# RWKV recurrence: block-diagonal state, zero-padded inverses and chunk products on alternate halves of the columns

## The chip, the cores and the metric

The kernel runs on one core of a Trainium2 chip. The metric is the device time of one execution in microseconds; lower is better. Each time is a median of several executions.

## The reference

The model has two transformer-like layers (a mixer and a feed-forward part each), and then two more layers of other kinds. It works on 512 tokens of width 1024. The mixer of each of the first two layers is made of three parts that read the same projection: RWKV7, retention, and latent attention. The change is in RWKV7, which has 4 heads of 64 channels and this recurrence over the tokens:

```
def step(state, inp):
    rt, kt, vt, wt, kkt, at = inp
    sa = jnp.einsum('bhvk,bhk->bhv', state, -kkt)
    state = (state * wt[:, :, None, :] + sa[..., None] * (kkt * at)[:, :, None, :]
             + vt[..., None] * kt[:, :, None, :])
    return state, jnp.einsum('bhvk,bhk->bhv', state, rt)
```

The output of a token is a matrix-vector product with a 64x64 state of each head; the state decays by channel, loses what an old key held, and gains the new value.

## The kernel before

The recurrence is computed in 8 chunks of 64 tokens (`CH`, `NCH`). Channels of two heads stand on the 128 partitions: head 2p + e is in tile p, on partitions 64e to 64e + 63. `rwkv_front` makes, for each chunk, `ar` (removal keys and receptances, scaled by decays) and `bk` (their counterparts), each 64 channels by 2 x 64 columns for a head.

- `rwkv_scores` forms, for each chunk and head, the 128x128 masked score matrix `g` of bk and ar (tile gps, 64 rows by 128 columns; the four products of one bank have the same e). It sends the 32x32 diagonal blocks to DRAM (SP's and POOL's queues), and transposes bk (`bkt`) and the values (`uv`) to token-major form.
- `rwkv_inverse` inverts 32 strictly lower triangular 64x64 matrices: a substitution of 31 steps on VectorE in 32x32 blocks, a way through DRAM (`s2`, then `tt`: 4 DMAs, two from SP's queue and two from ScalarE's), and a merge in four groups (tile mrg: 32x32 products, all in rows 0 to 63 and columns 0 to 31).
- `rwkv_chunk` runs 8 times in order. bch = scores x values + ar x state; copy to SBUF; uch = inverse x bch; copy into `uv`; mch = bkt x uv, from which with the decay `gam` the next state (`mst`) is made; ych = output. The products are in float32, for which each matmul stands as two instructions in the trace. bch and uch put all heads on output partitions 0 to 63; the products with the state use 64 rows (the head's channels), the others 128. mch and ych put heads of e = 0 and e = 1 on alternate halves of the output partitions.

All this runs beside the other two parts of the mixer. In `attn` the helper `weave` emits, after each step of `main` (retention, latent attention), 1.9 steps of `side` (scores, inverse, chunks), with a priority of 600 (`SPRI`). A scheduler orders each engine's queue before the run from priorities and a model of costs; engines then run their queues in order. Tiles of one tag share slots: tag R, with 26 slots of 128x512, holds most of the recurrence's tiles. Banks of PSUM have the tags pd, pt, pr and pa with two each; the recurrence uses pr. Dense products (tile pd, line 366) split weights and activations into a high and a low part, in three products each.

Of the kernel before, what the change touches and what calls it, by code (L numbers as in the profile page):

```python
# [5 lines left out]
F32 = mybir.dt.float32  # L6
# [9 lines left out]
P = 128  # L16
T = 512
# [19 lines left out]
# how far ahead of the program's order: loads and splits of weights, of small ones, products leaving their banks,  # L37
# reciprocal roots, the recurrence
WPRI, SMPRI, EPRI, CPRI, SPRI = 300, 0, 200, 500, 600
# first loads: block of x before which the second unit of weights comes, rank of the splits, who squares and adds blocks of x  # L40
START, AHEAD, VSQ, VACC = 3, -300, (5, 7), (6,)
# attention: steps of the recurrence per step beside it; steps of the retention after which latent values and queries follow;
# steps of the latent attention by which values wait, queries come early, and after which the recurrence's output follows; banks
WEAVE, VAT, QAT, VDELAY, QAHEAD, RPOST = 1.9, (2, 6, 10, 14), 6, 1, 3, 20
MSCB, MOB, DB0, DB1, DB2 = ("pa", "pr", "pa", "pr"), "pd", ["pd", "pt"], ["pd"], ["pd"]
# end of the even layer: products after which weights of the odd layer are split, places of the sums and roots, delay of the fourth product
EARLY, SEAM, LATE, AH2, AH3 = (3, 5), (3, 1, 5, 5, 1), 2, -300, -250
# odd layer: steps of the gates after each product, steps of what runs beside values and output gates
# [28 lines left out]
def _constants():  # L77
# [34 lines left out]
    # decays of the retention, split between queries and keys about the middle token  # L112
# [16 lines left out]
def _layout(inp):  # L129
    """Every array as the chip reads it; only permutations, slices, copies and zero padding."""  # L130
# [15 lines left out]
    for l in range(L2):  # L146
# [10 lines left out]
        # retention's values beside the latent keys' rotary part, three blocks of rows to a unit  # L157
# [61 lines left out]
class _Kernel:  # L219
# [7 lines left out]
    def t(self, name, tag, dt=F32):  # L227
        """a [128, T] tile; tags share slots in the order in which their tiles are written first"""
        if tag in KEPT:
            return self.tp.tile([P, T], dt, tag=tag, name=name, bufs=KEPT[tag])  # L230
        return self.php.tile([P, T], dt, tag=tag, name=name, bufs=self.phb[tag])

    def phase(self, name, **tags):
        """memory of one phase: tag -> number of [128, T] slots"""
# [21 lines left out]
    def pd(self, name="pd"):  # L256
        """a bank for a dense product, in turn from the tags that the phase has set aside"""
        self.turn += 1
        return self.bank(self.dbanks[self.turn % len(self.dbanks)], name)
# [70 lines left out]
    def wbits(self, src, tags, n=UNIT, ahead=0):  # L330
        """a unit of weights in tiles of the phase: (k, columns) -> (hi, lo)"""
# [28 lines left out]
    def evac(self, out, ps, y):  # L360
        """a dense product times y, ahead of other work so that its bank is free again"""
# [6 lines left out]
    def mm3(self, out, a, b, first, last):  # L368
        """out += a^T b, both operands as exact (hi, lo) pairs."""
# [21 lines left out]
    def rsqrt_(self, x, n, key, bias, more, floor):  # L391
# [12 lines left out]
        # a step of third order, then one of Newton's  # L404
# [11 lines left out]
    def col_sums(self, ps, c0, sq, rhs, first=True, last=True):  # L416
        """ps[:, c0 + tb*n ...] = sum over partitions of sq, token-major."""
# [4 lines left out]
    def spread(self, r, ps):  # L422
        """r: [128 tokens, token blocks] -> psum [128 features, tokens]"""
# [4 lines left out]
    def spread_heads(self, r, ps, tag):  # L428
        """r: [128 tokens, token blocks * two heads] -> psum [64 features of each head, T]"""
# [49 lines left out]
    def softplus(self):  # L479
        """4 softplus(-lam)"""  # L480
# [24 lines left out]
    def rope_angles(self):  # L505
        """cos and sin of both rotations, on [32 * token block + frequency, token], kept in DRAM as
# [1323 lines left out]
```

## Time and profile before

| | |
|---|---|
| time, median of 3 runs | 2117.26 us (2115.75 to 2122.51) |
| profiled execution, span (its only time) | 2118.6 us |
| TensorE busy | 98% |
| VectorE, ScalarE, GpSimd busy | 60%, 38%, 3% |
| granted TensorE clock, mean | 0.961 |

A TensorE clock of 1.00 is 2.4 GHz and 0.50 is 1.2 GHz. In rows, `128*64 128x64` means a stationary operand of 128 rows and 64 columns and a moving one of 128 rows by 64; PE is TensorE's matmul part, DVE is VectorE, ACT is ScalarE, SP is the queue of SyncE. Matmuls are pipelined: the length of one runs on under the next, so the step from start to start is what one costs.

### The profile page before, as it was taken

Reading aid. Unit: us, or ns where it says so; the run is one execution under the profiler, and the core shown is the slowest. Engines: PE = TensorE matmul, PEld = TensorE weight load, DVE = VectorE, ACT = ScalarE, POOL = GpSimd, SP = SyncE. Lnnn points to the kernel's source line nnn. Section 1 sums busy time; section 2 is a strip of 40 time slices with the busy share of each in tenths; the row PEclk is TensorE's granted clock in tenths of the full one; section 3 lists DMA queues with packets and bytes.
Section 4 is the critical chain, followed back from the end, with each engine's and each line's share of the span. In section 5 each row is a group of like instructions: output and inputs, shape, how many; then the busy total and the mean of one; then the engine's idle time right before and its main releaser. Section 6 shows DMA issues by size and latency. Waiting matters only on the chain.

```text
span 2118.6 us, 25896 instructions
## 1 busy us (share of the span) xinstructions
PE 2086.5 (98%) x10080; PEld 1662.8 (78%) x10080; DVE 1277.1 (60%) x2387; ACT 805.6 (38%) x1315; POOL 66.1 (3%) x112
## 2 busy tenths in 40 slices
PE   8999999999999999999999999999999999999998
PEld 5787667888888877776678888888788888878786
DVE  7963176553544678623755445346988885388565
ACT  6421164322322444213643223225554544347242
POOL 3100000000000011000000000000000000020000
PEclk9986699999999999958999999999999999999999
DMA  5320022332333333201222323333333323222121
GB/s 184 107 64 13 28 59 74 97 96 93 100 100 96 124 113 105 64 5 32 67 88 92 100 91 98 100 95 90 98 96 93 102 95 103 101 69 90 50 90 40
DMA packets 64782, 180.06 MB, mean 85 GB/s; under 512 B 13764, under 2 KB 16612, under 8 KB 64660
## 3 DMA queue, kind: packets, MB, share of 16 engines
q1 hardware_dynamic: 60464, 175.27, 26.9%
q0 software_dynamic: 1808, 2.69, 0.5%
q8 instruction: 79, 1.29, 0.3%
q10 hardware_dynamic: 2388, 0.45, 0.2%
q14 instruction: 43, 0.35, 0.1%
HBM read 172.29 MB, written 6.09 MB: 84 GB/s over the span
## 4 chain that ended last, share of the span: by engine, by line
PE 45%; DVE 4%; ACT 2%; DMA 1%; issue 1%; DVEq 0%; ACTq 0%
PE pd L366 39%; PE egate L366 1%; PE mo L366 1%; DVE wl L285 1%; PE oo L366 1%; PE msc L366 1%; PE ost L366 1%; DVE xl L303 0%; ACT wh L306 0%; DVE h L285 0%; PE osb L366 0%; ACT oe L306 0%; PE osf L366 0%; PE mpt L1145 0%; DMA wr<-ewin 0%
## 5 line engine op out<-in xcount | busy, mean ns | idle before, releaser
L366 PE MATMUL pd<-xh,wh 128*128 128x512 f32 (+1 forms) x1512 | 591.6, 391 | 6.4 <-ACT xh L306 6.4
L366 PE MATMUL pd<-xl,wh 128*128 128x512 f32 (+1 forms) x1512 | 592.8, 392 | 4.4 <-DVE xl L303 3.9
L366 PE MATMUL pd<-xh,wl 128*128 128x512 f32 (+1 forms) x1512 | 589.9, 390 | 0.0
L306 ACT ACTIVATE wh<-wr 128x1024 fp32r<-128x1024 f32 (+3 forms) x285 | 296.4, 1040 | 763.4 <-PE pd L366 524.5
L285 DVE TENSOR_TENSOR wl<-wr,wh 128x1024 fp32r<-128x1024 f32 (+3 forms) x285 | 341.7, 1199 | 102.0 <-ACT wh L306 100.8
L366 PEld LDWEIGHTS pd<-xl,wh 128*128 128x128 f32 (+1 forms) x1512 | 284.0, 188 | 67.2 <-DVE xl L303 8.6
L366 PEld LDWEIGHTS pd<-xh,wh 128*128 128x128 f32 (+1 forms) x1512 | 284.2, 188 | 65.5 <-ACT xh L306 7.2
L366 PEld LDWEIGHTS pd<-xh,wl 128*128 128x128 f32 (+1 forms) x1512 | 284.1, 188 | 57.6 <-issue 1.0
L366 PE MATMUL pd<-fal,wh 128*128 128x512 f32 x352 | 137.2, 390 | 0.0
L366 PE MATMUL pd<-fah,wl 128*128 128x512 f32 x352 | 137.0, 389 | 0.0
L366 PE MATMUL pd<-fah,wh 128*128 128x512 f32 x352 | 136.6, 389 | 0.0
L285 DVE TENSOR_TENSOR h<-pd,h 128x512 f32<-128x512 f32 x64 | 44.2, 691 | 150.1 <-PE pd L366 150.1
L366 PE MATMUL pd<-mxh,wh 128*128 128x512 f32 (+1 forms) x272 | 102.8, 378 | 0.0
L366 PE MATMUL pd<-mxh,wl 128*128 128x512 f32 (+1 forms) x272 | 102.6, 377 | 0.0
L366 PE MATMUL pd<-mxl,wh 128*128 128x512 f32 (+1 forms) x272 | 102.5, 377 | 0.0
L285 DVE TENSOR_TENSOR fth<-pd,RH 128x512 f32<-128x512 f32 x44 | 30.4, 692 | 118.6 <-PE pd L366 118.6
L285 DVE TENSOR_TENSOR fz<-pd,RB 128x512 f32<-128x512 f32 x44 | 30.4, 692 | 99.3 <-PE pd L366 99.3
L366 PEld LDWEIGHTS pd<-fal,wh 128*128 128x128 f32 x352 | 66.1, 188 | 14.3 <-DVE fal L285 0.6
L366 PEld LDWEIGHTS pd<-fah,wl 128*128 128x128 f32 x352 | 66.1, 188 | 13.7
L366 PEld LDWEIGHTS pd<-fah,wh 128*128 128x128 f32 x352 | 66.1, 188 | 13.6
L366 PEld LDWEIGHTS pd<-mxl,wh 128*128 128x128 f32 x272 | 51.2, 188 | 9.3
L366 PEld LDWEIGHTS pd<-mxh,wl 128*128 128x128 f32 x272 | 51.2, 188 | 9.2
(507 smaller groups left out, 3038.3 us busy)
## 6 DMA issues: line engine op xcount, KB each, us to landing
wr<-wgu SPq DMA_DIRECT2D x88, 512.0 KB, 3.5
wr<-ewin SPq DMA_DIRECT2D x48, 512.0 KB, 3.5
wr<-win SPq DMA_DIRECT2D x35, 512.0 KB, 3.5
wr<-wd SPq DMA_DIRECT2D x32, 512.0 KB, 3.6
wr<-wout SPq DMA_DIRECT2D x16, 512.0 KB, 3.5
wr<-ewout SPq DMA_DIRECT2D x16, 512.0 KB, 3.8
wr<-wd SPq DMA_DIRECT2D x16, 384.0 KB, 3.2
h<-xT SPq DMA_DIRECT2D x16, 256.0 KB, 4.7
```

Source lines behind the costliest of these rows:

```text
L285: (eng or self.nc.vector).tensor_tensor(out, x, y, op)
L306: self.nc.scalar.activation(out, x, f, **kw)
L366: self.nc.tensor.matmul(out=out, lhsT=lhsT, rhs=rhs, start=start, stop=stop)
```

## The change

The state of two heads becomes a block-diagonal 128x128 tile (`mbd`, two of them in turn), whose other blocks are set to zero once a layer. The inverses lie in `tt` with the heads of e = 0 on partitions 0 to 63 and those of e = 1 on 64 to 127, and the other half is zero. Thereby every product of a chunk has 128 rows by 64 columns, and successive products belong to e = 0 and e = 1, on alternate halves of the output partitions. bch has one bank and one copy; uch's result is copied in two halves, on VectorE and on ScalarE. The new state is (mch + state) x decay, in two adds and two multiplies of 64 partitions. The scores of e = 0 and e = 1 alternate, in two banks. `tt` comes back from DRAM in 8 DMAs, and the merge takes all 16 matrices of each e at once, the two e in alternation on different corners of the array, with three tiles of tag R. The diff also drops comments and docstrings everywhere; its core:

```diff
+        st = {"v": [], "ar": [], "bk": [], "rk": []}
+        st["gam"] = self.s("gam", 2 * NCH)[:].rearrange("p (c q) -> p c q", q=2)
...
-            g = self.s(f"gam{p}", NCH)
-            nc.vector.tensor_copy(g, e1[:].rearrange("p (c t) -> p c t", t=CH)[:, :, CH - 1])
-            st["gam"].append(g)
+            nc.vector.tensor_copy(st["gam"][:, :, p], e1[:].rearrange("p (c t) -> p c t", t=CH)[:, :, CH - 1])
...
+    def rwkv_memory(self, st):
+        st["tt"] = self.php.tile([P, 32, CH], F32, tag="tt", name="tt", bufs=1)
+        self.nc.gpsimd.memset(st["tt"], 0.0)
+        st["mbd"] = []
+        for i in range(2):
+            m = self.php.tile([P, 2 * P], F32, tag=f"mbd{i}", name="mbd", bufs=1)
+            self.nc.gpsimd.memset(m, 0.0)
+            st["mbd"].append(m[:].rearrange("p (q v) -> p q v", v=P))
     def rwkv_scores(self, l, st):
         nc = self.nc
         s1 = self.dr.tile([2, 32, 32, 32], F32, tag="s1", name="s1")
         st["g"] = []
         mask = self.co("mg").unsqueeze(1).to_broadcast([P, 4, P])
+        self.rwkv_memory(st)
         for cp in range(NCH // 2):
-            row = []
-            for e in range(2):
-                sl = slice(64 * e, 64 * e + 64)
-                ps = self.pr("gps")
-                for i in range(4):
-                    c, p = 2 * cp + i // 2, i % 2
+            row, pss = [], [self.pr("gps") for _ in range(2)]
+            for i in range(4):
+                c, p = 2 * cp + i // 2, i % 2
+                for e in range(2):
+                    sl = slice(64 * e, 64 * e + 64)
                     lh = st["bk"][p][c // 4][sl, c % 4].rearrange("p s t -> p (s t)")
                     rh = st["ar"][p][c // 4][sl, c % 4].rearrange("p s t -> p (s t)")
-                    self.mm(ps[:, i * P:(i + 1) * P], lh, rh, True, True)
+                    self.mm(pss[e][:, i * P:(i + 1) * P], lh, rh, True, True)
+            for e in range(2):
                 g = self.t("g", "R")
                 g3 = g[:].rearrange("p (h t) -> p h t", t=P)
-                self.mul(g3, ps[:].rearrange("p (h t) -> p h t", t=P), mask)
+                self.mul(g3, pss[e][:].rearrange("p (h t) -> p h t", t=P), mask)
                 row.append(g3)
                 for b, q in enumerate((nc.sync, nc.gpsimd)):
                     d = slice(32 * b, 32 * b + 32)
-                    q.dma_start(out=s1[b, 8 * cp + 4 * e:8 * cp + 4 * e + 4].rearrange("h j t -> j h t"), in_=g3[d, :, d])
+                    m = 16 * e + 4 * cp
+                    q.dma_start(out=s1[b, m:m + 4].rearrange("h j t -> j h t"), in_=g3[d, :, d])
...
-        tt = self.php.tile([P, 32, CH], F32, tag="tt", name="tt", bufs=1)
-        nc.gpsimd.memset(tt[32:64, :, 0:32], 0.0)
+        tt = st["tt"]
         s2 = self.dr.tile([P, 16, 32], F32, tag="s2", name="s2")
         nc.sync.dma_start(out=s2, in_=x3)
-        for hf in range(2):
-            for b, q in enumerate((nc.sync, nc.scalar)):
-                o, i = 64 * hf + 32 * b, 32 * b + 16 * hf
-                q.dma_start(out=tt[i:i + 16, :, 32 * b:32 * b + 32], in_=s2[o:o + 32].rearrange("c i t -> i c t"))
-        tts = [tt[:, 8 * g:8 * g + 8] for g in range(4)]
-        st["tt"] = tts
-        for g in range(4):
-            n21 = self.php.tile([P, 256], F32, tag="q1k", name="n21", bufs=3)
-            n3 = n21[:, :256].rearrange("p (c t) -> p c t", t=32)
-            t11 = self.php.tile([P, 256], F32, tag="q1k", name="t11", bufs=3)
-            t3 = t11[:, :256].rearrange("p (c t) -> p c t", t=32)
-            for e in range(2):
-                nc.vector.transpose(out=n3[32:64, 4 * e:4 * e + 4], in_=st["g"][g][e][0:32, :, 32:64])
-            nc.vector.transpose(out=t3[0:32], in_=tts[g][0:32, :, 0:32])
-            ps = self.pr("mrg")
-            for i in range(8):
-                self.mm(ps[0:32, 32 * i:32 * i + 32], n3[32:64, i], tts[g][32:64, i, 32:64], True, True)
-            w = self.php.tile([P, 256], F32, tag="q1k", name="mrgw", bufs=3)
-            self.act(w[0:32, :256], ps[0:32, :256])
-            ps = self.pr("mrg2")
-            for i in range(8):
-                self.mm(ps[0:32, 32 * i:32 * i + 32], t3[0:32, i], w[0:32, 32 * i:32 * i + 32], True, True)
-            self.act(tts[g][0:32, :, 32:64], ps[0:32, :256].rearrange("p (c t) -> p c t", t=32))
-            yield
+        for e in range(2):
+            for hf in range(2):
+                for b, q in enumerate((nc.sync, nc.scalar)):
+                    o, i = 64 * hf + 32 * b + 16 * e, 64 * e + 32 * b + 16 * hf
+                    q.dma_start(out=tt[i:i + 16, 16 * e:16 * e + 16, 32 * b:32 * b + 32], in_=s2[o:o + 16].rearrange("c i t -> i c t"))
+        n21 = self.t("n21", "R")[:].rearrange("p (c t) -> p c t", t=32)
+        t11 = self.t("t11", "R")[:].rearrange("p (c t) -> p c t", t=32)
+        w = self.t("mrgw", "R")[:].rearrange("p (c t) -> p c t", t=32)
+        half = [(slice(64 * e, 64 * e + 32), slice(64 * e + 32, 64 * e + 64), slice(16 * e, 16 * e + 16)) for e in range(2)]
+        for e, (up, dn, own) in enumerate(half):
+            for g in range(4):
+                nc.vector.transpose(out=n21[dn, 4 * g:4 * g + 4], in_=st["g"][g][e][0:32, :, 32:64])
+            nc.vector.transpose(out=t11[up], in_=tt[up, own, 0:32])
+        pss = [self.pr("mrg") for _ in range(2)]
+        for i in range(16):
+            for e, (up, dn, own) in enumerate(half):
+                self.mm(pss[e][up, 32 * i:32 * i + 32], n21[dn, i], tt[dn, 16 * e + i, 32:64], True, True)
+        for e, (up, dn, own) in enumerate(half):
+            self.act(w[up], pss[e][up].rearrange("p (c t) -> p c t", t=32))
+        yield
+        pss = [self.pr("mrg2") for _ in range(2)]
+        for i in range(16):
+            for e, (up, dn, own) in enumerate(half):
+                self.mm(pss[e][up, 32 * i:32 * i + 32], t11[up, i], w[up, i], True, True)
+        for e, (up, dn, own) in enumerate(half):
+            self.act(tt[up, own, 32:64], pss[e][up].rearrange("p (c t) -> p c t", t=32))
+        yield
 
     def rwkv_chunk(self, l, st, c):
         nc = self.nc
         if c == 0:
             st["y"] = [self.t("yrw", "R"), self.t("yrw", "R")]
-            st["m"] = None
-        UV, TT = st["uv"][c], st["tt"][c // 2]
-        G = [[st["g"][c // 2][e][:, 2 * (c % 2) + p] for p in range(2)] for e in range(2)]
-        M = st["m"]
-        b = self.php.tile([P, 256], F32, tag="q1k", name="bsb", bufs=3)
-        for e in range(2):
-            sl = slice(64 * e, 64 * e + 64)
-            ps = self.pr("bch")
-            for p in range(2):
-                h = 2 * p + e
-                o = ps[0:64, p * 64:p * 64 + 64]
-                self.mm(o, G[e][p][:, 0:64], UV[:, h * 64:h * 64 + 64], True, M is None)
-                if M is not None:
-                    self.mm(o, st["ar"][p][c // 4][sl, c % 4, 0], M[sl, p, :], False, True)
-            nc.vector.tensor_copy(b[0:64, e * P:e * P + P], ps[0:64, :P])
+        UV, first = st["uv"][c], c == 0
+        M, Mn = st["mbd"][c % 2], st["mbd"][(c + 1) % 2]
+        sl = [slice(0, 64), slice(64, 128)]
+        def G(p, e):
+            return st["g"][c // 2][e][:, 2 * (c % 2) + p]
+        def V(p, e):
+            return UV[:, (2 * p + e) * 64:(2 * p + e) * 64 + 64]
+        ps = self.pr("bch")
+        for p in range(2):
+            o = slice(p * 64, p * 64 + 64)
+            for e in range(2):
+                self.mm(ps[sl[e], o], G(p, e)[:, 0:64], V(p, e), True, first)
+            if not first:
+                for e in range(2):
+                    self.mm(ps[sl[e], o], st["ar"][p][c // 4][:, c % 4, 0], M[:, p, sl[e]], False, True)
+        b = self.php.tile([P, P], F32, tag="q1k", name="bsb", bufs=2)
+        nc.vector.tensor_copy(b, ps[:, :P])
         ps = self.pr("uch")
-        for h in range(4):
-            p, e = divmod(h, 2)
-            self.mm(ps[0:64, h * 64:h * 64 + 64], TT[0:64, 4 * e + 2 * (c % 2) + p], b[0:64, e * P + p * 64:e * P + p * 64 + 64], True, True)
-        nc.vector.tensor_copy(UV[0:64], ps[0:64, :256])
+        for p in range(2):
+            for e in range(2):
+                self.mm(ps[sl[e], p * 64:p * 64 + 64], st["tt"][:, 16 * e + 2 * c + p], b[:, p * 64:p * 64 + 64], True, True)
+        uv3 = UV.rearrange("p (q e v) -> p q e v", e=2, v=64)
+        p3 = ps[:, :P].rearrange("p (q v) -> p q v", v=64)
+        nc.vector.tensor_copy(uv3[0:64, :, 0], p3[0:64])
+        self.act(uv3[0:64, :, 1], p3[64:128])
         if c < NCH - 1:
             ps = self.pr("mch")
-            for h in range(4):
-                p, e = divmod(h, 2)
-                self.mm(ps[64 * e:64 * e + 64, p * 64:p * 64 + 64], st["bkt"][p][c // 4][:, c % 4, 64 * e:64 * e + 64],
-                        UV[:, h * 64:h * 64 + 64], True, True)
-            Mn = self.sp.tile([P, 2, 64], F32, tag="mst", name="mst")
             for p in range(2):
-                gm = st["gam"][p][:, c:c + 1]
-                if M is None:
-                    self.ts(Mn[:, p], ps[:, p * 64:p * 64 + 64], gm)
-                else:
-                    mg = self.sp.tile([P, 64], F32, tag=f"mg{p}", name="mg")
-                    self.ts(mg, M[:, p], gm)
-                    self.stt(Mn[:, p], ps[:, p * 64:p * 64 + 64], gm, mg, ALU.mult, ALU.add)
-            st["m"] = Mn
+                for e in range(2):
+                    self.mm(ps[sl[e], p * 64:p * 64 + 64], st["bkt"][p][c // 4][:, c % 4, 64 * e:64 * e + 64], V(p, e), True, True)
+            p3 = ps[:, :P].rearrange("p (q v) -> p q v", v=64)
+            gm = st["gam"][:, c].unsqueeze(2).to_broadcast([P, 2, 64])
+            if first:
+                for e in range(2):
+                    self.mul(Mn[sl[e], :, sl[e]], p3[sl[e]], gm[sl[e]])
+            else:
+                new = self.sp.tile([P, 2, 64], F32, tag="mst", name="mst")
+                for e in range(2):
+                    self.add(new[sl[e]], p3[sl[e]], M[sl[e], :, sl[e]])
+                for e in range(2):
+                    self.mul(Mn[sl[e], :, sl[e]], new[sl[e]], gm[sl[e]])
         ps = self.pr("ych")
-        for h in range(4):
-            p, e = divmod(h, 2)
-            sl = slice(64 * e, 64 * e + 64)
-            o = ps[sl, p * 64:p * 64 + 64]
-            self.mm(o, UV[:, h * 64:h * 64 + 64], G[e][p][:, 64:128], True, M is None)
-            if M is not None:
-                self.mm(o, M[sl, p, :], st["ar"][p][c // 4][sl, c % 4, 1], False, True)
+        for p in range(2):
+            o = slice(p * 64, p * 64 + 64)
+            for e in range(2):
+                self.mm(ps[sl[e], o], V(p, e), G(p, e)[:, 64:128], True, first)
+            if not first:
+                for e in range(2):
+                    self.mm(ps[sl[e], o], M[:, p, sl[e]], st["ar"][p][c // 4][:, c % 4, 1], False, True)
         for p in range(2):
             self.act(st["y"][p][:, c * CH:c * CH + CH], ps[:, p * 64:p * 64 + 64])
```

## Rows read from the trace of the kernel before

**Rows 1.** The page: busy time of each engine; granted clock in 40 slices.
```profile
PE 2086.5 (98%) x10080; PEld 1662.8 (78%) x10080; DVE 1277.1 (60%) x2387; ACT 805.6 (38%) x1315; POOL 66.1 (3%) x112
...
PEclk9986699999999999958999999999999999999999
```
**Rows 2.** Windows: stretch, length, busy by engine (instructions), clock, DMA share, GB/s.
```profile
146.78:184.32 37.54, 37.54 (x260) 29.32 (x257) 9.92 (x29) 8.89 (x24) 0.00 (x0) 0.50 0.03 8
...
894.30:965.98 71.68, 71.68 (x339) 51.38 (x339) 13.97 (x43) 7.74 (x24) 0.00 (x0) 0.50 0.02 6
sum 160.42, PE 160.42 PEld 116.56 DVE 33.66 ACT 22.34 POOL 0.12; mean PE 53.47 PEld 38.85 DVE 11.22 ACT 7.45 POOL 0.04
```
**Rows 3.** Windows of one tile: bch in those stretches; bch, uch, mch, ych throughout.
```profile
sum 160.42, PE 34.91 PEld 24.05 DVE 6.78; mean PE 11.64 PEld 8.02 DVE 2.26
...
0.00:2118.60 2118.60, 43.94 (x240) 30.63 (x240) 9.04 (x32) 0.96 0.28 85
...
0.00:2118.60 2118.60, 20.31 (x128) 14.85 (x128) 6.67 (x16) 0.96 0.28 85
...
0.00:2118.60 2118.60, 9.17 (x112) 6.75 (x112) 6.66 (x28) 0.96 0.28 85
...
0.00:2118.60 2118.60, 43.02 (x240) 31.19 (x240) 5.41 (x32) 0.96 0.28 85
```
**Rows 4.** Timeline of TensorE, layer 0, low clock: start, length, instruction.
```profile
201.40 0.70 PE L366 MATMUL mch<-uv,bkt 128*64 128x64 f32 x8
201.88 0.42 PE L366 MATMUL ych<-g,uv 128*64 128x64 f32 x2
...
205.06 0.58 PE L366 MATMUL rkv<-rv,rkt 128*128 128x128 f32 x1
```
**Rows 5.** Timeline of TensorE, layer 1, high clock, first and second chunk.
```profile
884.27 0.45 PE L366 MATMUL mch<-uv,bkt 128*64 128x64 f32 x8
884.55 0.40 PE L366 MATMUL ych<-g,uv 128*64 128x64 f32 x8
884.89 0.41 PE L366 MATMUL pd<-wh,xl 128*128 128x320 f32 x1
...
889.92 0.28 PE L366 MATMUL ych<-g,uv 128*64 128x64 f32 x2
...
891.92 0.41 PE L366 MATMUL pd<-wl,xh 128*128 128x320 f32 x1
```
**Rows 6.** Windows of one tile, the whole span: mrg, gps.
```profile
0.00:2118.60 2118.60, 11.62 (x256) 10.20 (x256) 5.75 (x16) 0.96 0.28 85
...
0.00:2118.60 2118.60, 15.23 (x128) 12.77 (x128) 10.64 (x16) 0.96 0.28 85
```
**Rows 7.** Timeline of TensorE, layer 1, the merge.
```profile
878.16 0.59 PE L366 MATMUL mrg<-mrgw,t 32*32 32x32 f32 x13
878.56 0.21 PE L366 MATMUL mrg<-tt,n 32*32 32x32 f32 x1
...
878.68 0.57 PE L366 MATMUL mrg<-tt,n 32*32 32x32 f32 x13
```
**Rows 8.** Groups by tile: VectorE's copies and state update, ns min/median/max.
```profile
L871 DVE COPY bsb<-bch x32: 281/283/284, 156.3 to 955.3; 64x128 f32<-64x128 f32 x32
...
L876 DVE COPY uv<-uch x16: 415/417/417, 161.1 to 957.9; 64x256 f32<-64x256 f32 x16
...
L303 DVE SCALAR_TENSOR_TENSOR mst<-mch,gam,mg x24: 274/280/285, 172.2 to 947.9; 128x64 f32<-128x64 f32 x24
```
**Rows 9.** Issues of the inverses' DMAs (ns); a wait of TensorE (us).
```profile
L831 SPq DMA_DIRECT2D tt<-s x4: 326/402/479, 139.3 to 863.9; - x4
...
PE mrg L366 <- DMA tt<-s: 1.5, 1, 1.5
```
**Rows 10.** Windows after the recurrence in both layers, all engines.
```profile
249.18:330.00 80.82, 79.64 (x401) 54.38 (x400) 55.05 (x152) 46.47 (x118) 3.85 (x6) 1.00 0.23 64
...
965.98:1050.00 84.02, 83.22 (x431) 57.69 (x430) 48.99 (x143) 46.81 (x115) 4.88 (x8) 1.00 0.18 55
```

More of the change, by code (lines that the diff above doesn't have):

```diff
@@ L615, in rwkv_front @@
         nc, pk, pj = self.nc, self.pk, {}
-        st = {"v": [], "ar": [], "bk": [], "gam": [], "rk": []}
+        st = {"v": [], "ar": [], "bk": [], "rk": []}
+        st["gam"] = self.s("gam", 2 * NCH)[:].rearrange("p (c q) -> p c q", q=2)
         def proj(m):
```

## Prediction

> **What bounds the kernel now.** I read the page's busy times first: TensorE 98% busy, the next engine 60% [rows 1]. So time is TensorE's own, and a change is worth what it takes off TensorE's queue. The granted clock over the slices comes second: it falls to 6 in slices 4 and 5 and to 5 and 8 in 18 and 19 [rows 1], where the RWKV recurrence of the two layers stands. The windows come third: 160.4 us run at clock 0.50 (1.2 of 2.4 GHz) with TensorE busy in every microsecond [rows 2], so this is slow work, not waiting. Last I asked which tiles hold it: the products of the recurrence (bch, uch, mch, ych) are 720 instructions and 43.94 + 20.31 + 9.17 + 43.02 = 116.4 us busy, of bch 34.91 of 43.94 us at the low clock [rows 3]. "Busy" counts the pipelined end of a product, which lies under its successor, so I price by start-to-start steps.
>
> **The chunk products, before.** There are 8 chunks in each of two layers. From the second chunk on ych is 16 instructions in four times two pairs: 128 rows by 64 columns, then 64 by 64. It takes 201.88 to 205.06 = 3.18 us at the low clock and 889.92 to 891.92 = 2.00 at the high one [rows 4, 5]; bch has the same form. At the low clock are 34.91 / 3.18 = 11.0 of bch's sets and at the high one 9.03 / 2.00 = 4.5, a share of 0.71. So 14 chunks x 2 products x (0.71 x 3.18 + 0.29 x 2.00 = 2.84) = 79.5 us, and some 2.5 for the two first chunks, which have no state: 82, against 87 busy. I scale uch alike, 20.31 x 82 / 87 = 19. mch already puts its heads on alternate column halves: 8 instructions in 0.48 us low, 0.28 high, so 14 x 0.42 = 6. Together 107 us.
>
> **After.** The instructions stay 48 a chunk; each is now 128 rows by 64 columns and its neighbour sits on the other half of the columns. The trace has that form: mch and the first chunk's ych, 16 instructions, take 884.27 to 884.89 = 0.62 us, 39 ns each, at the high clock, and mch 60 ns at the low one [rows 4, 5]. The zero rows add no columns to stream. 720 x 39 = 28 us: **79 us saved**; with the clock as before 720 x (0.71 x 60 + 0.29 x 39) = 39, 68 saved.
> The Trainium skill ("TensorE: Matmul & The Clock Gate", section "Wait — 56ns, not 53.3ns?") speaks against so fast a pace: with the hardware's decoding off a matmul costs the sequencer some 62 ns, which binds when the array's work is shorter. By that 720 x 62 = 45 us, and the forecast would be 17 us later; the 39 ns of the row decide, and I keep 28.
>
> **Merge and scores.** The merge's 256 small products (11.62 us busy [rows 6]) now alternate between the corners of the array. Where two kinds on different rows alternated by chance, six took 878.56 to 878.68, 20 ns each, against 31 for the 13 before [rows 7]. 256 x 20 = 5; I take **5 us saved** (bounds 0 and 7). The scores gps (128 instructions, 15.23 us [rows 6]) alternate between the two row halves and two banks. No row shows this form; the nearest is again the 31 to 20 ns. Bounds: no gain, and half, 7.6; I take **5**, by the ratio.
>
> **The rest of the low-clock stretches.** Of the 160.4 us, 0.79 x 107 = 85 and some 5 of the merge are the recurrence; 70 are dense and retention products. If the clock stays up, products that stream columns halve and pairs go by 2.00 / 3.18 = 0.63; I take 0.55, **31 us saved**. I count on the clock because of what TensorE did before it fell at 894.3 [rows 2]: sets of pairs that switch between two shapes, as those of [rows 5]. These sets are gone, and of what took 2.00 us some 0.6 is left between dense products at whose pace the clock stood at 1.00. It is not certain (rival 1).
>
> **What is added.** (a) The copy of bch is one of 128x128 instead of two of 64x128 (0.28 each); that of uch is split into 64x128 on VectorE (0.42 now for 64x256) and one on ScalarE; the state takes two adds and two multiplies of 64x128 instead of 4 operations of some 0.28 [rows 8]. VectorE is even; ScalarE gets 16 copies, at VectorE's 0.28 some 5 us, under TensorE's other work. But the chain bch, copy, uch, copy, mch, state has three hand-overs a chunk and less product time beside them, and the copy on ScalarE can queue behind a split of weights. Dense products fill them now. From nothing to 26 us (all bare: two copies and four state steps at 0.28, 1.7, and three tails of 0.45 - 0.28, 0.5 [rows 5, 8], less the 0.6 of ych, 1.6 x 16); I take **8 lost**. (b) The inverses come back in 8 DMAs a layer instead of 4, half on SP's queue, half on ScalarE's: two more issues of 0.4 on each [rows 9], with all that stands behind them there. TensorE waited 1.5 us for the last one in layer 0 [rows 9]: **1 lost**, bounds 0 and 2 for each layer. (c) In layer 0 the clock was down from 146.78, before the first chunk, after that wait and the first small merge products [rows 2, 9]; I leave 14 us at the low clock, **7 lost** (bounds 0 and 0.45 x 37.54 = 17, the whole of that stretch). (d) Memory sets on POOL, 3% busy [rows 1], run before the scores and ahead of POOL's DMAs of them; behind that lies the substitution, covered by dense products: nothing, up to 2 us without cover. (e) Three merge tiles move into the group of 26 slots: no row shows a wait for one there; nothing, and at most a merge some us later, under the same cover. One decay tile for two: nothing.
>
> **Sum.** 79 + 5 + 5 + 31 - 8 - 1 - 7 = 104 us. The profiled execution's span is 2118.6 us, the only time it has; 1.3 above the median of 2117.3, within the runs' 2115.75 to 2122.51. 2118.6 - 104 - 1.3 = **2013 us**.
>
> **Rivals.** *1, the clock stays low* in the chunks. For it: in 894.3 to 965.98 dense products stood between the chunks and did not lift it [rows 2]. Against: what filled the queue then is gone. Then 68 + 3 (merge) + 5 - 1 = 75, and hand-overs are covered as now: 2042. The skill's rule (same page, "Why this matters for your kernels") puts a fall down to gaps in which TensorE idles; by it nothing in this change lifts the clock, and the time would be this rival's. The trace disagrees in part: there was no gap in 71.68 us at 0.50 [rows 2]. *2, bare hand-overs.* The chain sets the chunk's pace: 26 instead of 8 us, 2031. For it: three waits on other engines a chunk; against: the same waits cost TensorE nothing visible now. *3, the halves don't overlap* in products that accumulate in one bank, so it doesn't do what it says: uch's 19 us for 128 is 148 ns each, x 720 = 107, nothing saved: 2118. Against: the rows of mch. *4, slower.* Freed of the recurrence, retention and attention stand alone on TensorE, gaps open there and the clock falls in what follows, 249.18 to 330 and 965.98 to 1050, 163 us busy at 1.00 [rows 10]. All of it at half adds 163 x (1 / 0.55 - 1) = 133; it is slower than before once more than 75 / 133 = 0.56, some 92 us, run low; two thirds of it give 2042 + 89 = 2131. Against: they stand alone there already, at 1.00.
>
> **Chances.** Forecast 0.62, with a range of its own of 1994 (no loss by clock and hand-overs) to 2033; rival 1 0.18, rival 2 0.10, rival 3 0.05, rival 4 0.05. The range 1994 to 2052 holds the forecast, rivals 1 and 2 with some spread and leaves rivals 3 and 4 and the tails out. What can be told from no change is 0.3%, 6 us: faster 0.90, same 0.05 (rival 3), slower 0.05 (rival 4).
>
> **What would show it.** 16 ych instructions in about 0.6 us at clock 1.00; the four chunk products some 30 to 40 us busy instead of 116; low clock for under 20 us instead of 160, and none in layer 1; gps and mrg together down by some 10; new TensorE waits for bsb, uv and the state under 10 us in all. Wrong it is if the low stretches remain as long in chunks (rival 1), or if a chunk's products still take 100 ns each (rival 3).

## The result, and the profile after

The changed kernel takes 2023.66 us (median of 4 runs, 2022.66 to 2024.76), the kernel before, beside it, 2116.69 (4 runs, 2115.75 to 2122.51): a ratio of 0.9567, 95% interval 0.953 to 0.9604. The forecast was 2013, its range 1994 to 2052. The time lies 11 us above the forecast. The forecast had the right sign and nearly the right size. For the pace of the chunk products it named only a part of the reason: the experiments show that the shapes of neighbours count for more than the halves of the columns.

The page of the changed kernel, busy time and granted clock, against [rows 1]:

```profile
PE 1987.4 (98%) x10080; PEld 1591.8 (79%) x10080; DVE 1275.4 (63%) x2367; ACT 808.3 (40%) x1323; POOL 68.7 (3%) x116
...
PEclk9999999999999999999999999999999999999999
```

TensorE has as many instructions as before and 99 us less to do; no slice of the clock row is below 9. The windows of the two stretches inside the kernel that are left at the low clock, against [rows 2]:

```profile
107.92:111.34 3.42, 3.39 (x8) 2.71 (x9) 3.42 (x8) 2.21 (x3) 0.00 (x0) 0.50 0.52 153
1756.56:1759.97 3.41, 3.41 (x18) 3.41 (x18) 3.23 (x13) 0.82 (x2) 0.99 (x1) 0.50 0.02 6
```

6.8 us instead of 160.4, none of it in a chunk. The windows of one tile over the whole span, in the order bch, uch, mch, ych, mrg, gps, against [rows 3, 6]:

```profile
0.00:2020.90 2020.90, 15.08 (x240) 10.99 (x240) 4.67 (x16) 1.00 0.29 89
...
0.00:2020.90 2020.90, 7.36 (x128) 5.15 (x128) 4.53 (x16) 4.40 (x16) 1.00 0.29 89
...
0.00:2020.90 2020.90, 9.87 (x112) 6.42 (x112) 8.09 (x28) 1.00 0.29 89
...
0.00:2020.90 2020.90, 11.61 (x240) 9.88 (x240) 5.41 (x32) 1.00 0.29 89
...
0.00:2020.90 2020.90, 7.21 (x256) 6.55 (x256) 4.71 (x8) 1.00 0.29 89
...
0.00:2020.90 2020.90, 12.44 (x128) 10.55 (x128) 10.28 (x16) 1.00 0.29 89
```

The four chunk products are busy for 43.9 us instead of 116.4. The timeline of TensorE in one chunk of layer 1 (start, length, instruction), against [rows 5]:

```profile
842.16 0.30 PE L366 MATMUL pd<-wl,xh 128*128 128x320 f32 x1
842.39 0.33 PE L366 MATMUL mch<-uv,bkt 128*64 128x64 f32 x2
842.65 0.41 PE L366 MATMUL pd<-wh,xl 128*128 128x320 f32 x1
842.99 0.39 PE L366 MATMUL mch<-uv,bkt 128*64 128x64 f32 x5
843.16 0.22 PE L366 MATMUL ych<-g,uv 128*64 128x64 f32 x1
...
843.83 0.42 PE L366 MATMUL pd<-wh,xh 128*128 128x320 f32 x1
```

The 16 products of ych (and the last one of mch among them) take 843.16 to 843.83, 0.67 us instead of 2.00. But mch is cut in two by a dense product: from 842.39 to 842.99 two small products and one dense one take 0.60 us, where two at 35 ns [rows 5] and a dense one at its own pace of 0.15 (842.01 to 842.16 just before) would be 0.22. TensorE's largest new waits (engine, line, what for: us in all, times, longest):

```profile
PE pd L366 <- DVE mz L285: 2.3, 1, 2.3
...
PE bkt L787 <- DVE rk L285: 1.0, 1, 1.0
```

The first of them, in the timeline of layer 0:

```profile
105.21 0.30 DVE L851 STREAM_TRANSPOSE n<-g 32x128 f32<-32x128 f32 x1
...
105.80 1.22 DVE L285 TENSOR_TENSOR wl<-wr,wh 128x1024 fp32r<-128x1024 f32 x1
...
107.21 0.69 DVE L285 TENSOR_TENSOR mz<-pd,RB 128x512 f32<-128x512 f32 x1
...
107.95 0.79 PE L366 MATMUL pd<-xh,wh 128*128 128x512 f32 x1 [2.29 <-DVE mz L285]
```

The eight transposes of n21 now stand in one piece of VectorE's queue between the first steps of the substitution (the last at 105.21); the evacuation mz comes late, TensorE stands still for 2.29 us, and the clock is low from 107.92 to 111.34.

### The profile page after: what moved, and what is told of

Same layout as the page of the kernel before. It is cut to its first block, busy times and chain, and to the rows that moved or that the text cites. A ratio compares the mean times of both kernels' runs of the same rounds, so it can differ in the third digit from the quotient of the medians.

```text
span 2020.9 us, 25875 instructions
## 1 busy us (share of the span) xinstructions
PE 1987.4 (98%) x10080; PEld 1591.8 (79%) x10080; DVE 1275.4 (63%) x2367; ACT 808.3 (40%) x1323; POOL 68.7 (3%) x116
## 4 chain that ended last, share of the span: by engine, by line
PE 83%; DVE 8%; issue 4%; ACT 3%; DMA 2%; POOL 1%; SPq 0%; DVEq 0%; ACTq 0%; POOLq 0%
PE pd L366 69%; PE msc L366 2%; PE mo L366 2%; DVE wl L285 1%; PE egate L366 1%; PE ro L366 1%; PE oo L366 1%; PE mpt L1169 1%; PE bch L366 1%; ACT wh L306 1%; DVE xl L303 1%; PE ost L366 1%; DVE h L285 0%; ACT oe L306 0%; DVE xinv L285 0%
## 5 line engine op out<-in xcount | busy, mean ns | idle before, releaser
L366 PEld LDWEIGHTS pd<-fal,wh 128*128 128x128 f32 x352 | 66.1, 188 | 14.5 <-DVE fal L285 0.7
```

What stands on the lines that cost most here:

```text
L366: self.nc.tensor.matmul(out=out, lhsT=lhsT, rhs=rhs, start=start, stop=stop)
```

## The experiments

Differences of a few microseconds are read against the unaltered change on the same chip, where it was timed beside them; beside the first four runs (same halves, 64 rows, late transposes, scores by head) it was not, and only their ratios to the kernel before can be compared with its 0.9567. "Start to start" is the time from each matmul's start to that of the next, summed by tile; a single such time is called a step.

**Column halves or shapes?** My theory was that neighbours on different column halves overlap. The first run was to take just that away.

```diff
-        for p in range(2):
-            ...
-            for e in range(2):
+        for e in range(2):
+            for p in range(2):
```

> The changed kernel with the loops of the four chunk products turned round: all products of one head parity (one column half) first, then those of the other; shapes, zero padding and counts stay. Theory (neighbours on different column halves overlap, and that is the main gain): the 720 chunk instructions go from 49 ns each (35 us) to the 95 ns that the old u products took at full clock on one half, 68 us or more, so about 2057 us; if the slower products also bring the low clock back, up to 2100 us. Rival (one shape throughout is the gain, the halves don't matter): still about 50 ns each, within 5 us of 2024.

Measured 2023.26 us, ratio to before 0.9577 (0.9543 to 0.9612), against the change's own 0.9567. The 720 products take 37.4 us start to start instead of 35.1. TensorE's timeline of one mch and ych:

```profile
836.75 0.46 PE L366 MATMUL mch<-uv,bkt 128*64 128x64 f32 x8
837.03 0.28 PE L366 MATMUL ych<-g,uv 128*64 128x64 f32 x2
837.15 0.28 PE L366 MATMUL ych<-ar,mbd 128*64 128x64 f32 x2
837.27 0.33 PE L366 MATMUL ych<-g,uv 128*64 128x64 f32 x4
837.38 0.34 PE L366 MATMUL ych<-ar,mbd 128*64 128x64 f32 x4
837.55 0.28 PE L366 MATMUL ych<-g,uv 128*64 128x64 f32 x2
837.67 0.28 PE L366 MATMUL ych<-ar,mbd 128*64 128x64 f32 x2
837.88 0.41 PE L366 MATMUL pd<-wh,xh 128*128 128x320 f32 x1
```

The edit took only a part of the overlap away. Its eight mch still take 0.28 us, as in [rows 5]: the first, at 836.75, is bound to VectorE's copy of uv and the second, 13 ns later, to ScalarE's, so products of the two halves start side by side although the edit puts them four instructions apart. uch (6.1 us for all 128, 6.2 in the changed kernel) is no slower either. In ych eight of the 16 run so, in 0.28 us (837.27 to 837.55); the other eight stand alone on their half, at steps of 58 ns, and the set takes 0.85 us instead of 0.67. So this run can't price the halves by its time. Its steps can, together with a row of the kernel before, the old uch, which has one shape and one half throughout:

```profile
888.22 0.56 PE L366 MATMUL uch<-bsb,tt 64*64 64x64 f32 x6
888.71 0.41 PE L366 MATMUL pd<-wh,xl 128*128 128x320 f32 x1
```

Its first step is 0.11 us and its last 0.15, the four between are 58 ns each. On alternate halves two products take 59 ns together (in the whole groups below, four take 0.12). Sixteen of one shape on one half would thus take some 16 x 58 + 140 (the two ends) = 1070 ns, an estimate, against 610 on alternate halves. The theory holds, but for some 0.46 us of the step from 2.00 to 0.67, not for all of it.

**The shape alone.** The state's products get 64 rows again; the order of all instructions is the same as in the changed kernel.

```diff
-    self.mm(ps[sl[e], o], st["ar"][p][c // 4][:, c % 4, 0], M[:, p, sl[e]], False, True)
+    self.mm(ps[sl[e], o], st["ar"][p][c // 4][sl[e], c % 4, 0], M[sl[e], p, sl[e]], False, True)
...
-    self.mm(ps[sl[e], o], M[:, p, sl[e]], st["ar"][p][c // 4][:, c % 4, 1], False, True)
+    self.mm(ps[sl[e], o], M[sl[e], p, sl[e]], st["ar"][p][c // 4][sl[e], c % 4, 1], False, True)
```

> The changed kernel with the state's products on 64 rows again (the head's own half of the operand and of the state tile), everything else the same, the order of all instructions too; 224 of the 720 chunk products change their shape. Theory (a change of shape between neighbours costs time on TensorE): bch and ych go from 23 us to the 28 to 40 us that about 20 to 70 ns for each of the 224 would add, so 2029 to 2040 us. Rival (only the column half matters): within 2 us of 2024, bch and ych still 23 us. A clock that falls in the chunks would speak for full rows as what keeps it up.

Measured 2035.5 us, ratio 0.9643 (0.9601 to 0.9684). One bch in its timeline:

```profile
840.52 0.34 PE L366 MATMUL bch<-uv,g 128*64 128x64 f32 x4
840.78 0.33 PE L366 MATMUL bch<-mbd,ar 64*64 64x64 f32 x4
841.05 0.34 PE L366 MATMUL bch<-uv,g 128*64 128x64 f32 x4
841.31 0.33 PE L366 MATMUL bch<-mbd,ar 64*64 64x64 f32 x4
841.57 0.41 PE L366 MATMUL pd<-wh,xl 128*128 128x320 f32 x1
```

Each group of one shape takes 0.26 us with four products in it, and took 0.25 with two in the old set (2.00 us for eight groups). The four stand on both halves, two at a time, and the two on one half, one behind the other: two steps of 58 ns either way. The other 0.14 us of a group are the price of the change of shape. bch and ych go from 23.2 to 34.4 us start to start; 28 sets with three changes more at 0.14 would be 11.8 (an estimate). The clock stays at 1.00 in the chunks.

**Both old features.** The two edits above together give the old pairs back, in bch and ych alone; uch and mch stay as in the changed kernel.

> The changed kernel with both features of the old bch and ych put back at once: one column half after the other, and the state's products on 64 rows, so that pairs of 128 by 64 and of 64 by 64 take turns as before the change. Theory, formed after the first four runs (each change of shape between neighbours costs about 0.14 us, the column halves nothing): a pair takes the 0.26 us of the old trace, bch and ych of a chunk 2.0 us each, 57 us in all instead of 23, so 2058 us; if the slow pairs bring the low clock back, as before the change, up to 2095. Rival (a shape change costs only what the run with 64 rows alone showed, 11 us, whatever the order): 2035 us.

Measured 2099.8 us, ratio 0.9911 (0.9873 to 0.9949): of the 93 us that the change gains, 75 are lost again (against the unaltered change beside it, 2024.88). Its timeline in layer 1, and its windows at the low clock:

```profile
877.63 0.33 PE L366 MATMUL bch<-uv,g 128*64 128x64 f32 x2
877.89 0.32 PE L366 MATMUL bch<-mbd,ar 64*64 64x64 f32 x2
878.14 0.33 PE L366 MATMUL bch<-uv,g 128*64 128x64 f32 x2
```

```profile
173.03:241.29 68.26, 68.26 (x316) 44.95 (x315) 14.08 (x44) 10.25 (x29) 1.22 (x2) 0.50 0.02 7
886.41:927.37 40.96, 40.96 (x205) 29.56 (x203) 9.53 (x26) 7.21 (x20) 0.00 (x0) 0.50 0.04 12
941.03:951.27 10.24, 10.24 (x49) 7.91 (x48) 2.80 (x12) 2.06 (x6) 0.14 (x1) 0.50 0.00 0
```

Between this run and the one with 64 rows only the order of the products of bch and ych differs: a set has eight groups instead of four, and no two products of it side by side. A pair takes 0.26 us as before the change, and the low clock is back in the chunks, 119.5 us of it, with TensorE busy in all of them. That shows both halves of the new theory: a change of shape costs TensorE 0.14 us beside the steps of the products, and sets of such pairs bring the clock down. Whether it is the number of changes that does so or the slow pace of the whole set (2.0 us instead of 1.05) is not separated. In the profiled run, 79 us above the change's own, the chunk products take 59 us more start to start and all else 20. The Trainium skill ("TensorEngine Tiling (Array Packing)", section "Key Properties") says that a change of the tiling mode, not of the tile alone, drains TensorE; the 0.14 us agree. My prediction didn't weigh that rule.

**No shape of their own.** If each change of shape costs, the form of the dense products should be better still. The u and m products first:

```diff
-    self.mm(ps[sl[e], p * 64:p * 64 + 64], st["tt"][:, 16 * e + 2 * c + p], b[:, p * 64:p * 64 + 64], True, True)
+    self.mm(ps[:, p * 64:p * 64 + 64], st["tt"][:, 4 * c + 2 * p:4 * c + 2 * p + 2].rearrange("k e t -> k (e t)"), b[:, p * 64:p * 64 + 64], True, True)
...
-    self.mm(ps[sl[e], p * 64:p * 64 + 64], st["bkt"][p][c // 4][:, c % 4, 64 * e:64 * e + 64], V(p, e), True, True)
+    self.mm(ps[:, p * P:p * P + P], st["bkt"][p][c // 4][:, c % 4], UV[:, p * P:p * P + P], True, True)
```

> The changed kernel with uch and mch at 128 rows by 128 columns, the form of the dense products beside them: the inverses of two heads side by side as one block-diagonal operand for uch, all 128 columns of the keys against all 128 of the values for mch, of which the diagonal blocks are read. 120 instructions instead of 240. Theory (a change between 128x64 and 128x128 costs too): uch and mch fall from 11.9 to about 6 us, and the dense product behind each group starts 0.1 us earlier at two sides of some 45 groups, another 5 to 9: 2009 to 2014 us. Rival (such a change costs nothing, and mch streams twice the columns): 2 to 3 us from uch alone, 2021 us, and the product after a group is as late as now.

Measured 2022.48 us, ratio 0.9544 (0.9512 to 0.9575); the unaltered change beside it 2024.88, 0.9562 (0.9523 to 0.96): not to be told apart. Its timeline:

```profile
840.37 0.31 PE L366 MATMUL pd<-wh,xh 128*128 128x320 f32 x1
840.52 0.55 PE L366 MATMUL uch<-bsb,tt 128*128 128x64 f32 x4
840.88 0.39 PE L366 MATMUL pd<-wl,xh 128*128 128x320 f32 x1
841.11 0.31 PE L366 MATMUL pd<-wh,xl 128*128 128x320 f32 x1
...
841.75 0.71 PE L366 MATMUL mch<-uv,bkt 128*128 128x128 f32 x4
842.39 0.34 PE L366 MATMUL ych<-g,uv 128*64 128x64 f32 x4
```

The way in costs nothing now (840.37 to 840.52, 0.15, a dense product's own pace), but the first dense product behind uch still takes 0.23. And mch pays for its columns: four products of 128 columns take 0.64 us (0.11 each of the steps between them, the rest at the two ends), where eight of 64 took 0.28 [rows 5]. Fewer instructions of more columns are no gain.

All four products so, with score tiles laid out by chunk and a doubled state operand for bch (its core):

```diff
+    self.mm(ps[:, full[p]], flat(g3[:, 0, 2 * p:2 * p + 2]), UV[:, full[p]], True, first)
+    if not first:
+        self.mm(ps[:, full[p]], st["ard"][:, p, c % 4], M[:, p], False, True)
...
+    self.mm(ps[:, full[p]], UV[:, full[p]], flat(g3[:, 1, 2 * p:2 * p + 2]), True, first)
+    if not first:
+        self.mm(ps[:, full[p]], M[:, p], two(ar[p][:, 1]), False, True)
```

> All four chunk products at 128 rows by 128 columns, as in the run with uch and mch, and bch and ych too: score tiles laid out by chunk so that two heads' columns stand side by side, the state's operand for bch doubled by POOL, diagonal blocks read. 360 instructions instead of 720, none with a shape of its own. It also adds: a copy of 128x256 for bch instead of 128x128, four small copies of y instead of two, score masks in smaller pieces, 8 more transposes of n21. Theory (shape changes are the price): 360 x 55 to 60 ns = 20 to 22 us instead of 35, and about 10 us off the dense neighbours: 1998 to 2006 us. Rival (with so little product time in a chunk the hand-overs between engines lie bare): TensorE waits for bsb, uv and the state of 10 us or more, 2015 us or above.

Measured 2041.12 us, ratio 0.9626 (0.9589 to 0.9664), 16 slower than the change. The 360 products take 45.9 us start to start, 127 ns each, instead of 720 at 49. Another part is waiting, for which the smaller pieces that VectorE got are a likely reason that no run isolates:

```profile
PE pd L366 <- DVE mz L285: 9.3, 2, 6.7
```

The rival's number came true, for another reason: not the hand-overs of the chunk (1.0 us of waits for bsb and the state) but columns, and the same mz as above. The profiled run also has 17.06 us at the low clock from 1897.91 on, long after the recurrence, where no window of the unaltered change is longer than 3.4; why is open.

**Whole groups.** The first product into a bank becomes the one whose operand comes last, so nothing slips between.

```diff
-            for e in range(2):
-                self.mm(ps[sl[e], o], G(p, e)[:, 0:64], V(p, e), True, first)
             if not first:
-                for e in range(2):
-                    self.mm(ps[sl[e], o], st["ar"][p][c // 4][:, c % 4, 0], M[:, p, sl[e]], False, True)
+                for e in (1, 0):
+                    self.mm(ps[sl[e], o], st["ar"][p][c // 4][:, c % 4, 0], M[:, p, sl[e]], True, False)
+            for e in (1, 0):
+                self.mm(ps[sl[e], o], G(p, e)[:, 0:64], V(p, e), first, True)
...
-                for e in range(2):
+                for e in (1, 0):
                     self.mm(ps[sl[e], p * 64:p * 64 + 64], st["bkt"][p][c // 4][:, c % 4, 64 * e:64 * e + 64], V(p, e), True, True)
```

> The changed kernel with the products of bch and mch in an order in which the first of a bank is the one whose operand comes last: state products ahead of score products, second head ahead of the first. Then no dense product slips in between: one group instead of two or three for each of bch and mch. Theory (each passage from a dense product to a small one and back costs 0.2 us, whatever the shape): 30 to 40 passages less, chunk products 35 to about 30 us and the dense ones behind them 2 to 3 us, 5 to 8 us less than the changed kernel beside it. Rival (the groups wait longer for their last operand, TensorE's order being fixed): waits for the state or uv of 5 us or more, no gain.

Measured 2016.69 us (6 runs, 2013.72 to 2021.07), ratio 0.9518 (0.9491 to 0.9545); the unaltered change beside it 2024.6 (2022.41 to 2025.44). The 7.9 us less are as the theory had it, and this version beats both kernels. Its timeline, and the only wait of its matmuls for a chunk's operand:

```profile
831.61 0.34 PE L366 MATMUL bch<-mbd,ar 128*64 128x64 f32 x4
831.77 0.29 PE L366 MATMUL bch<-uv,g 128*64 128x64 f32 x4
831.89 0.29 PE L366 MATMUL bch<-mbd,ar 128*64 128x64 f32 x4
832.00 0.29 PE L366 MATMUL bch<-uv,g 128*64 128x64 f32 x4
832.22 0.41 PE L366 MATMUL pd<-wh,xh 128*128 128x320 f32 x1
```

```profile
PE bch L366 <- DVE mbd L285: 2.0, 7, 0.6
```

16 products in 0.61 us; the 720 take 28.2 us, 39 ns each, against 35.1 us in the unaltered change. bch stands in 16 pieces instead of 29 and mch in 14 instead of 36.

**The transposes of n21.** Two ways to get them out of the substitution: a lower rank, or a tile of their own so that they run before it.

```diff
-                nc.vector.transpose(out=n21[dn, 4 * g:4 * g + 4], in_=st["g"][g][e][0:32, :, 32:64])
+                with self.tc.high_priority(-600): nc.vector.transpose(out=n21[dn, 4 * g:4 * g + 4], in_=st["g"][g][e][0:32, :, 32:64])
```

> The changed kernel with the eight VectorE transposes of the merge's n21 at a lower rank, so that they run at the end of the substitution and not between its first steps. Theory (they hold up the evacuation of a dense product on a full VectorE, and the clock falls after the gap): TensorE's wait for mz of 2.3 us and the low clock of 3.4 us near 107 us go, 4 us less, about 2020 us. Rival (VectorE is full in the whole stretch, the same work is late at another place): within 1 us of 2024, and a new wait of about 2 us stands elsewhere.

```diff
+        n21 = self.php.tile([P, T], F32, tag="n21", name="n21", bufs=1)[:].rearrange("p (c t) -> p c t", t=32)
+        ...
         x = self.t("xinv", "I")
...
-        b = self.php.tile([P, P], F32, tag="q1k", name="bsb", bufs=2)
+        b = self.php.tile([P, P], F32, tag="q1k", name="bsb", bufs=1)
```

> The changed kernel with a tile of its own for n21 (paid for with one buffer of bsb), so that its eight transposes run right behind the score masks, before the substitution. Theory (they hold up the evacuation mz inside the substitution, and the clock falls after the gap): the wait for mz of 2.1 to 2.8 us and the 3.4 us of low clock near 110 us go, 4 us less than the changed kernel timed beside it. Rival (VectorE is as full before the substitution, so the wait only moves): within 1 us of it, with a wait of TensorE of about 2 us elsewhere in the first 130 us.

Measured 2028.54 us (ratio 0.9603, 0.9567 to 0.964) for late, and for early 2028.38 (2027.23 to 2032.08) against 2024.6 beside it, where 4 us less was expected of both. The early one is slower, by 3.8 us; the late one is not faster, and its interval overlaps with the change's own (0.953 to 0.9604). In both the wait for mz and the low clock at 108 us are gone. In the late one TensorE waits 4.0 us for macc instead of 0.7; the low clock is elsewhere. The longest windows are two of the late and one of the early kernel:

```profile
128.48:135.31 6.83, 6.35 (x19) 5.38 (x20) 3.58 (x23) 0.40 (x1) 0.00 (x0) 0.50 0.13 48
831.62:841.87 10.25, 10.25 (x74) 7.76 (x73) 1.45 (x5) 2.22 (x7) 0.00 (x0) 0.50 0.01 2
```

```profile
150.11:163.76 13.65, 13.65 (x121) 10.68 (x114) 1.44 (x5) 3.09 (x8) 0.00 (x0) 0.50 0.01 2
```

So for the late transposes the rival's reason fits: VectorE is full in the whole stretch (9.1 to 9.8 of 10 us in each from 100 to 140 of the early kernel), and what is taken from one place is late at another. The early kernel has no new wait of some 2 us before 130 us, as the rival had it; its loss goes with the low clock. Two of the three windows run from the end of the merge through the first chunks, with TensorE busy throughout; what lets the clock fall there stays open.

> The changed kernel with both: early transposes and whole groups. Theory: the two savings add up, 9 to 12 us less than the changed kernel beside it, 2012 to 2015 us. Rival (what is saved at one place is waited for at another): no better than the better one of the two alone.

Early transposes and whole groups together: 2022.25 us (ratio 0.9543, 0.9516 to 0.9569). The savings don't add up: it is 5.6 us worse than whole groups alone, where early transposes alone cost 3.8. Here too the clock is low in the merge and the first chunks, for 10.24 us from 150.06 on.

**The scores by head.**

```diff
-            for i in range(4):
-                c, p = 2 * cp + i // 2, i % 2
-                for e in range(2):
+            for e in range(2):
+                for i in range(4):
+                    c, p = 2 * cp + i // 2, i % 2
```

> The changed kernel with the score products of one head parity after those of the other again, as before the change (two banks still). Theory (the row halves of neighbours overlap): the 128 score products go from 11.7 us to the 14.6 us of before, 3 us more, about 2027 us. Rival (the score products wait for their banks and inputs whatever their order): 11.7 us still, within 1 us of 2024.

The products take 14.5 us start to start instead of 11.7, as in the theory: alternating the heads on the row halves is worth 2.8 us. Yet the kernel takes 2022.92 us (ratio 0.9578, 0.9544 to 0.9611), no longer than the change (2023.66, 0.9567): VectorE's order shifted with it, and in this one the wait for mz and the low clock at 108 us are not there. The size of the effect is shown by its rows, not by the time.

**The yardsticks.**

> The changed kernel itself, unaltered, timed beside the three others on the same chip: about 2024 us. It is the yardstick for differences of a few microseconds.

> The changed kernel itself, unaltered, as the yardstick on the same chip: about 2024 us.

2024.88 us (4 runs, 2024.1 to 2029.74) and 2024.6 (6 runs, 2022.41 to 2025.44).

## Why the prediction was near, step by step

Terms of the sum, in us saved, against start-to-start sums of the two profiled executions:

| step | predicted | measured |
|---|---|---|
| chunk products | 79 (107 to 28) | 70 (105.5 to 35.1) |
| merge | 5 | 4 (10.8 to 6.8) |
| scores | 5 | 2.9 (14.6 to 11.7) |
| all else: 31 - 8 - 1 - 7 | 15 | 20.5 (1972.6 to 1952.1) |
| sum | 104 | 97.8 |

- **Chunk products, the reason.** "Its neighbour sits on the other half of the columns" is true, and less than half of the gain of a set. The term left out is the change of shape: seven changes fewer at 0.14 us are 1.0 of the 1.4 us between 2.0 and 0.61, the halves 0.46. The row that I read as a row on halves (mch and the first ych, 16 in 0.62 us) is one of a single shape too, so the forecast came out near for a reason that it didn't name. The rows to tell the two apart were there: the old uch, on one half without a change of shape, has steps of 58 ns, and the pairs of [rows 5] 0.25 us for two. Of the 70 us, some 32 are the clock (87 us of chunk products ran at 0.50, taken at 2.00 / 3.18), 28 the shape (28 sets), 17 the halves (28 sets, and 16 x 0.23 of uch), less 7 for cuts; these are estimates from the steps.
- **Rival 3** took 148 ns a product for halves that don't overlap. That mean holds the low clock and the ends of short groups; at 1.00 the step on one half is 58 ns. No run is without overlap altogether, but 16 products of bch that accumulate in one bank take 0.61 us in the whole groups, which rules the rival out.
- **Chunk products, the size.** 39 ns each holds for a whole set and is what the whole-group version has for all 720. In the changed kernel bch and mch are cut by dense products that slip in while the second head's operand is under way; that is the 7 us between 28.2 and 35.1. The prediction's rows showed sets without a cut, and it didn't ask how TensorE's order would fall.
- **The 62 ns of the Trainium skill** ("TensorE: Matmul & The Clock Gate", section "Wait — 56ns, not 53.3ns?") did not bind: 39 ns in the whole groups, as forecast.
- **Merge.** The size held (4 of 5 us), the reason by half. Only the 64 products in the middle of a layer's 128, where the two kinds of product alternate, go at 18 ns each (1.15 us); the first and the last 32 stand alone and take 1.12 us each, 35 ns, no less than before [rows 7]. That fits an order that takes one corner after the other there, though the kernel's loops alternate them; no run tests it.
- **The clock** rose in the chunks for the reason given: the pairs are gone, and with the pairs back it is low again. Rival 1 is out. Of the 20.5 us of "all else" this is the gain, less what was lost.
- **Losses.** They were put at 16 and are some 7 to 10. No run shows the gain of 31 by itself; with the old pairs back, 119.5 us of low clock made all else 20 us longer, which for 160 would be 27 (an estimate), and 27 to 31 less 20.5 is what was lost. Hand-overs, put at 8, show one wait of TensorE for a chunk's operand in the changed kernel, 0.2 us of bch for the first state; their price is the cuts, in the term above. Rival 2 is out: even with no cuts it is 2.0 us of waits of matmuls, and 2.6 of weight loads for ScalarE's copy of uv. The wait for the inverses' DMA (1.5 before [rows 9]) is gone, where 1 us more was forecast. No low clock is left where I put 14 us of it, from 146.78 on; but the two kernels with early transposes have 13.65 and 10.24 us just there, so it hangs on the order of the work and not on the change alone.
- **What I missed.** I put the merge's move at nothing "under the same cover". Its transposes are now free to run early, and VectorE, which I called even, has no room from 100 to 140 us: 2.3 us of waiting and 3.4 us of low clock, of which half (1.7) is lost. With the new wait for rk (1.0) and half of the window at 1756.56 (1.7) that makes 6.7 us that can be named; the rest stays unassigned.
- **Rival 4** did not come: after the recurrence one window of 3.41 us is low ahead of the span's last 5 us, not 92.
- **From span to time.** The terms are 6 us below the forecast's 104; 4 of the 11 us of the miss are none of them. I took the span of 2118.6 for a time and 1.3 off it. The changed kernel's profiled execution took 2022.66 us with a span of 2020.9, so its time is 1.8 above its span, and this execution lay 1.0 below the median.

## What to carry to other kernels

Count on TensorE steps and changes of shape, not instructions: a step is 58 ns here, for one product on one column half or for two on alternate halves, and a change between 128-row and 64-row products adds 0.14 us. Zero rows that make all shapes alike are cheaper than the array rows that they waste. Keep small products together: let the first into a bank be the one whose operand comes last, and no dense product cuts them. When a row serves as the price of a new form, ask which of its features the new form shares, and remove one at a time; then look in the trace whether the edit did remove it, since the order in which TensorE works need not be that of the loops.

## What the runs showed of the hardware

- At clock 1.00 the small float32 products on one column half take steps of 58 ns, and two on alternate halves 59 together: 16 in 0.61 us with both ends. Products of the two halves pair up even where four of one half are emitted first (mch of the first run).
- A change between 128x64 and 64x64 products adds 0.14 us: a group with two steps in it takes 0.26.
- Four 128x128 products of 128 columns take 0.64 us (steps of 0.11), eight of 128x64 and 64 columns 0.28.
- Between a dense product and uch in the same 128x128 shape the way in is free, and the way out costs 0.08 us (0.23 against 0.15).
- The clock was at 0.50 for 68.26 us with TensorE busy in all of it, in chunks that change shape 16 times in bch and ych; with half as many changes, and the halves side by side, it stayed at 1.00.
